# Transposes of branch c's merged sums packed four to a PSUM bank, and the final stores on one queue

## The chip, the core and the metric

One NeuronCore of a Trainium2 chip runs one decoder layer. The metric is device time in microseconds (us), the median of several executions. Engines are called PE (TensorE), ACT (ScalarE), DVE (VectorE), POOL (GpSimd) and SP (SyncE); each runs its own instruction stream in order, and semaphores join them.

## What is computed

The layer works on 256 tokens of width 2048 in float32. A mixer runs three token mixers a, b, c on the normalised input; each result is projected to width 2048, weighted by sigmoid gates and summed; the sum is projected once more and added to the input. A SwiGLU block and a last norm follow.

```python
m = (g[:, :, 0] * (ya @ w_br_a) + g[:, :, 1] * (yb @ w_br_b) + g[:, :, 2] * (yc @ w_br_c))
h = h + m @ w_out
h = h + (silu(rms(h) @ w_gate) * (rms(h) @ w_up)) @ w_down
out = rms_norm(h, norm_final)
```

## The kernel before

Every product is made in split precision: an operand is cut into a rounded high half (ACT, line 108) and the remainder (DVE, line 109) by `split`, and three matmuls stand for one (high by high, low by high, high by low). Weights come from HBM by SP's queue, 1 MB at a time, are cut in SBUF slots, and are multiplied in units. An ordinary unit (`KTiles`, lines 344 to 349) has 24 matmuls of 512 columns; the gates and the SwiGLU use a scheme with fewer products (`Squares`, line 451), whose units have 24 (kind N), 9 (kind Wp) or 12 (kind Ws) matmuls.

`run` writes out the order of the work by hand. Before it emits unit j it emits the cuts of units some way ahead; after the unit it calls `step_side`, which advances one of the waiting generators (`beside`) by one step. So every engine sees its part of a side step between the work of two units, and keeps that order.

Branch c is the third branch (b = 2). Its groups run as: gates of columns 0 and 1 as one `Squares` group, `br(0)`, `br(1)`, gates of columns 2 and 3 as one `Squares` group, `br(2)`, `br(3)`, then the four `output` groups that multiply by `w_out`. When `br(n)` ends, `after` (line 852) adds the gated product to the sums `m[n]` and puts the generator `turn` (line 846) beside the units. `turn` transposes the four 128-column K-tiles of `m[n]`, each for both halves of the tokens (t = 0, 1), so that they can be the stationary operand of `output`. It has two steps of two K-tiles. Each K-tile goes through `transposed` (line 245), which takes a PSUM bank, writes two transposes into half of it (line 249) and splits that half into the slabs of `mT` (lines 108 and 109, 128x256). Over n = 0 to 3 that makes eight steps, called T1 to T8 below: T1 and T2 (n = 0) and T3 and T4 (n = 1) fall between the units of the second gate group, T5 to T8 around `br(3)` and the first `output` group.

PSUM has eight banks, and all tiles of PSUM come from one pool of eight (`bank`, line 93). The pool hands out the bank that was released longest ago in program order; a tile is released when its last reader is done, and the first instruction that writes the new tile waits for that. A `Squares` group holds up to seven banks: a unit N opens four, the first Wp a fifth, the first Ws two more; they stay open until the group nears its end. The unit order of the second gate group is N, Wp, [T2], Ws, [T3], N, Wp, [T4], Ws and so on, with T1 ahead of the first Wp.

```python
def transposed(dst, srcs, scale=None):
    pt = bank()
    for t in range(NT):
        nc.tensor.transpose(pt[:, toks(t)], srcs[t], ident)
    split(*dst, pt[:, :SEQ], scale)
```

At the very end `final_norm` (line 997) is called for the first 128 tokens and then for two column halves of the other 128. When a token tile is done, its four column blocks are scaled, in the order 0, 1, 3, 2: blocks 0 and 3 by DVE (line 1016) and 1 and 2 by ACT (line 1018). Each is stored at once (line 1019, 256 KB): blocks 0 and 3 from SP's queue, 1 and 2 from ACT's.

Of the kernel before, what the change touches and what calls it, by code (L numbers as in the profile page):

```python
# [16 lines left out]
P = 128  # L17
# [13 lines left out]
NT = SEQ // P  # L31
# [20 lines left out]
def trunk(ctx: ExitStack, tc: tile.TileContext, x, norm_mix, norm_ffn, w_in, w_pool, pool_scale,  # L52
          w_br_a, w_br_b, w_br_c, w_out, w_gate, w_up, w_down, rel_bias, norm_final, out):
    nc = tc.nc
    x, out = x[0], out[0]
# [16 lines left out]
    def name(s):  # L72
        uid[0] += 1
        return f"{s}_{uid[0]}"

    def slot(shape, dt=F32):
        return slots.tile([P] + shape, dt, tag="slot", name=name("slot"))
# [4 lines left out]
    def open_late():  # L82

        early_ctx.close()
        late.append(ctx.enter_context(tc.tile_pool(name="late", bufs=3)))

    def wk(dt=F32):
        return work.tile([P, CH], dt, tag="wk", name=name("wk"), bufs=8)
# [4 lines left out]
    def bank():  # L93
        return psum.tile([P, CH], F32, tag="bank", name=name("bank"))

    def f32(ap):
        return ap.bitcast(F32)

    def cols(n):
        return slice(n * CH, (n + 1) * CH)  # L100

    def toks(t):
        return slice(t * P, (t + 1) * P)

    def split(hi, lo, src, scale=None):

        if scale is None:
            nc.scalar.activation(hi, src, AF.Copy)  # L108
            nc.vector.tensor_tensor(lo, src, f32(hi), OP.subtract)  # L109
        else:  # L110
            nc.scalar.activation(hi, src, AF.Copy, scale=scale)
            nc.vector.scalar_tensor_tensor(lo, src, scale, f32(hi), OP.mult, OP.subtract)
# [90 lines left out]
    ident = const.tile([P, P], F32, name="ident")  # L203
# [41 lines left out]
# [6 lines that stand above are left out]
# [14 lines left out]
    def beside(gen, after=2, lag=2):  # L265
        side.append([clock[0] + after, lag, gen])
# [13 lines left out]
    def finish_side():  # L280
        while side:
            clock[0] += 1
            step_side()
# [509 lines left out]
    mT, h, hT = [], [], []  # L793
    gates, m = {}, []
# [35 lines left out]
    def br(n, b, plain=False):  # L830
        key = ("ya", "yb", "yc")[b]

        def lhs():
            y = live[key]
            return lambda kt: (y[0][:, kt, :], y[1][:, kt, :])

        def before():
            if n == 0 and b == 0:
                finish_side()
                open_late()  # L840
                beside((xT.add_differences(p) for p in range(KT // 2)), after=4, lag=2)
            if n % 2 == 0 and b == 0:
                both = slot([2, NT, CH])
                m.extend([both[:, i, t] for t in range(NT)] for i in range(2))

        def turn():
            for j in range(4):
                transposed(mT[0](4 * n + j), [m[n][t][:, j * P:(j + 1) * P] for t in range(NT)])
                if j % 2:
                    yield  # L850

        def after(acc):
            if b == 2 and n == 0:
                mT.append(Halves())
            for t in range(NT):
                g = gates[n][t]
                if plain:
                    nc.scalar.activation(g, g, AF.Sigmoid)
                if b == 0:
                    nc.vector.tensor_mul(m[n][t], acc[t], g)  # L860
                else:
                    nc.vector.tensor_mul(g, acc[t], g)
                    nc.vector.tensor_add(m[n][t], m[n][t], g)
            if b == 2:
                beside(turn(), after=4 if n < 2 else 2, lag=1)

        return Group(lhs, range(HEADS), w_br[b], 0, n * CH, after, before, span=4 if b else 2)
# [98 lines left out]
    def down(part, n):  # L966
        f0, f1 = PARTS[part]
        last = part == len(PARTS) - 1
        cs = cols(n)

        def lhs():
            def tile(kt):
                assert kt // 4 in ready
                return act[kt // 4][:, kt % 4, :], act[kt // 4][:, 4 + kt % 4, :]
            return tile

        def before():
            if last and n == 0:
                load_gf()
                nc.scalar.preload_act_table(AF.Sqrt)  # L980

        def after(acc, t=None, c=slice(0, CH)):
            if t is not None:
                return final_norm(acc, t, c)
            for t in range(NT):
                nc.vector.tensor_add(h[t][:, cs], acc[t], h[t][:, cs])  # L986
                if last:
                    square_sum(st3[:, t, n:n + 1], h[t][:, cs])
                    nc.vector.tensor_mul(h[t][:, cs], h[t][:, cs], gf[0][:, cs])
            if last and n == 2:  # L990
                nc.vector.tensor_reduce(st3[:, :, 4], st3[:, :, 0:3], AX.X, OP.add)
                nc.vector.tensor_scalar(st3[:, :, 4], st3[:, :, 4], 1.0 / D_MODEL, EPS, OP.mult, OP.add)

        return Group(lhs, range(4 * f0, 4 * f1), w_down, f0 * CH, n * CH, after, before, staggered=last and n == 3,
                     span=4)

    def final_norm(acc, t, c):

        hc = h[t][:, 3 * CH + c.start:3 * CH + c.stop]
        a = [st3[:, t, k:k + 1] for k in range(10)]  # L1000
        nc.vector.tensor_add(hc, acc[:, c], hc)
        nc.scalar.activation(wk()[:, c], hc, AF.Square, accum_out=a[3])
        nc.vector.tensor_mul(hc, hc, gf[0][:, 3 * CH + c.start:3 * CH + c.stop])
        if c.stop < CH:
            nc.vector.scalar_tensor_tensor(a[4], a[3], 1.0 / D_MODEL, a[4], OP.mult, OP.add)
            return
        nc.scalar.activation(a[6], a[3], AF.Sqrt, scale=1.0 / D_MODEL, bias=a[4])
        nc.vector.scalar_tensor_tensor(a[5], a[3], 1.0 / D_MODEL, a[4], OP.mult, OP.add)
        nc.vector.reciprocal(a[7], a[6])
        nc.vector.scalar_tensor_tensor(a[8], a[7], a[7], a[5], OP.mult, OP.mult)  # L1010
        nc.vector.tensor_scalar(a[8], a[8], -0.5, 1.5, OP.mult, OP.add)
        nc.vector.tensor_mul(a[9], a[7], a[8])
        for n in (0, 1, 3, 2):
            hn = h[t][:, cols(n)]
            if n in (0, 3):
                nc.vector.tensor_scalar(hn, hn, a[9], None, OP.mult)
            else:
                nc.scalar.activation(hn, hn, AF.Copy, scale=a[9])
            (nc.sync if n in (0, 3) else nc.scalar).dma_start(out[toks(t), cols(n)], hn)

    groups = qkv("a", 0, start_block)
    groups += [channels("u", 3 * WIDTH, c, start_pooling if c else None) for c in range(2)]
# [7 lines left out]
    for part, (f0, f1) in enumerate(PARTS):  # L1030
        for f in range(f0, f1):
            groups += [swiglu(f, f == f1 - 1)]
        k = 2 if f1 - f0 > 2 else 3
# [43 lines left out]
```

## Time and profile before

| | us |
|---|---|
| median of 3 runs | 1565.94 |
| lowest, highest | 1565.84, 1566.08 |
| the profiled execution | 1565.91 |
| its span in the trace | 1564.1 |
| PE busy in the span | 1545.4 |
| DVE busy | 1093.8 |
| ACT busy | 746.3 |

The span runs from the first to the last instruction of the trace; the device time of that execution is 1.8 us longer. A row of the timeline gives start, duration, engine, line, operation, the tiles written and read, the shape and how many instructions were merged; in brackets stands the idle time before the row and what ended it. PEld is the loading of the stationary operand, which runs beside PE's matmuls.

### The profile page before, as it was taken

To read this page: it belongs to the slowest core of one execution; us is meant where nothing else is said; L and a number is where in the kernel's file an instruction comes from. 1 tells how busy PE (TensorE), PEld (TensorE's weight loads), DVE (VectorE), ACT (ScalarE), POOL (GpSimd) and SP (SyncE) were. 2 spreads that over 40 slices of the span, in tenths; PEclk is the share of its full clock that TensorE was granted. 3 is DMA by queue.
4 is the path that set the end of the run, shared out by engine and by line. 5 is a ranking of instruction groups with operands and counts; after the bars stand their busy time and mean duration, and the time that the engine had idled before them with its cause. 6 is when DMAs were issued, how large, how long until landed. Compare 5 with 4: busy or idle time off the path is not lost.

```text
span 1564.1 us, 19170 instructions
## 1 busy us (share of the span) xinstructions
PE 1545.4 (99%) x7895; PEld 1322.9 (85%) x7895; DVE 1093.8 (70%) x1064; ACT 746.3 (48%) x726; POOL 25.9 (2%) x94
## 2 busy tenths in 40 slices
PE   9999999999999999989999999999999999999997
PEld 9998999988888888878888878888888888888886
DVE  6453665644578888867666898667886769857685
ACT  7324343446545544635455545443554345544353
POOL 2000000101100000000000000000000000000000
PEclk9999999999999999999999999999999999999999
DMA  9655455554545655736654566555665555655551
GB/s 352 215 189 165 145 182 176 169 186 137 189 162 191 239 172 205 269 108 244 214 175 163 200 215 215 189 170 181 214 219 190 183 188 189 242 188 164 213 215 54
DMA packets 144456, 300.13 MB, mean 192 GB/s; under 512 B 6464, under 2 KB 8048, under 8 KB 144240
## 3 DMA queue, kind: packets, MB, share of 16 engines
q1 hardware_dynamic: 143024, 296.39, 55.6%
q10 hardware_dynamic: 1040, 1.45, 0.3%
q8 instruction: 62, 1.02, 0.3%
q0 software_dynamic: 304, 1.06, 0.2%
q14 instruction: 26, 0.21, 0.0%
HBM read 296.77 MB, written 2.11 MB: 191 GB/s over the span
## 4 chain that ended last, share of the span: by engine, by line
PE 96%; DVE 2%; ACT 1%; issue 0%; DMA 0%; ACTq 0%; DVEq 0%
PE bank L451 38%; PE bank L344 13%; PE bank L345 13%; PE bank L349 13%; PE bank L364 5%; PE bank L372 5%; PE bank L366 5%; DVE slot L109 1%; PE bank L951 1%; ACT slot L108 1%; PE bank L249 0%; PE bank L596 0%; DMA slot<-in_x_dram 0%; PE bank L597 0%; DVE slot L433 0%
## 5 line engine op out<-in xcount | busy, mean ns | idle before, releaser
L109 DVE TENSOR_TENSOR slot<-slot,slot 128x2048 fp32r<-128x2048 f32 (+3 forms) x406 | 719.0, 1798 | 187.3 <-ACT slot L108 186.8
L108 ACT ACTIVATE slot<-slot 128x2048 fp32r<-128x2048 f32 (+3 forms) x406 | 600.8, 1516 | 339.8 <-DVE slot L435 135.9
L451 PE MATMUL bank<-slot,slot 128*128 128x512 f32 x1719 | 441.3, 391 | 0.0
L451 PEld LDWEIGHTS bank<-slot,slot 128*128 128x128 f32 x1719 | 323.4, 189 | 67.0
L344 PE MATMUL bank<-slot,slot 128*128 128x512 f32 (+1 forms) x936 | 364.4, 390 | 0.0
L345 PE MATMUL bank<-slot,slot 128*128 128x512 f32 (+1 forms) x936 | 362.3, 388 | 0.0
L451 PE MATMUL bank<-slot,late 128*128 128x512 f32 x1014 | 279.4, 390 | 0.0
L349 PE MATMUL bank<-slot,slot 128*128 128x512 f32 (+1 forms) x936 | 236.5, 387 | 0.0
L451 PEld LDWEIGHTS bank<-slot,late 128*128 128x128 f32 x1014 | 189.6, 188 | 39.3 <-DVE slot L109 0.2
L344 PEld LDWEIGHTS bank<-slot,slot 128*128 128x128 f32 x936 | 175.8, 188 | 35.3
L345 PEld LDWEIGHTS bank<-slot,slot 128*128 128x128 f32 x936 | 175.9, 188 | 35.1
L349 PEld LDWEIGHTS bank<-slot,slot 128*128 128x128 f32 x936 | 174.9, 188 | 35.9
L364 PE MATMUL bank<-slot,slot 128*128 128x256 f32 x640 | 158.6, 286 | 0.0
L366 PE MATMUL bank<-slot,slot 128*128 128x256 f32 x640 | 156.9, 283 | 0.0
L366 PEld LDWEIGHTS bank<-slot,slot 128*128 128x128 f32 x640 | 122.8, 192 | 0.0
L364 PEld LDWEIGHTS bank<-slot,slot 128*128 128x128 f32 x640 | 122.7, 192 | 0.1
L372 PE MATMUL bank<-slot,slot 128*128 128x256 f32 x640 | 89.8, 283 | 0.0
L108 ACT ACTIVATE slot<-bank 128x512 fp32r<-128x512 f32 (+1 forms) x46 | 23.3, 520 | 132.0 <-PE bank L951 67.8
L372 PEld LDWEIGHTS bank<-slot,slot 128*128 128x128 f32 x640 | 82.6, 192 | 0.0
L109 DVE TENSOR_TENSOR slot<-bank,slot 128x512 fp32r<-128x512 f32 (+1 forms) x46 | 26.9, 595 | 59.4 <-ACT slot L108 59.4
L433 DVE TENSOR_TENSOR slot<-slot 128x1024 f32<-128x1024 f32 x49 | 59.7, 1218 | 0.0
L986 DVE TENSOR_TENSOR slot<-bank,slot 128x512 f32<-128x512 f32 x30 | 19.6, 686 | 55.5 <-PE bank L349 55.5
(160 smaller groups left out, 630.3 us busy)
## 6 DMA issues: line engine op xcount, KB each, us to landing
slot<-in_w_in_dram SPq DMA_DIRECT2D x103, 1024.0 KB, 5.1
slot<-in_w_gate_dram SPq DMA_DIRECT2D x88, 512.0 KB, 3.9
slot<-in_w_up_dram SPq DMA_DIRECT2D x88, 512.0 KB, 4.8
slot<-in_w_down_dram SPq DMA_DIRECT2D x44, 1024.0 KB, 5.1
slot<-in_w_out_dram SPq DMA_DIRECT2D x16, 1024.0 KB, 5.1
slot<-in_w_br_a_dram SPq DMA_DIRECT2D x8, 1024.0 KB, 5.1
slot<-in_w_br_b_dram SPq DMA_DIRECT2D x8, 1024.0 KB, 5.1
slot<-in_w_br_c_dram SPq DMA_DIRECT2D x8, 1024.0 KB, 5.1
```

Source lines behind the costliest of these rows:

```text
L108: nc.scalar.activation(hi, src, AF.Copy)
L109: nc.vector.tensor_tensor(lo, src, f32(hi), OP.subtract)
L344: nc.tensor.matmul(acc[:, c], hi[:, toks(t)], whi[:, j, c], start=i + j == 0, stop=False)
L345: nc.tensor.matmul(acc[:, c], lo[:, toks(t)], whi[:, j, c], start=False, stop=False)
L349: nc.tensor.matmul(acc[:, c], hi[:, toks(t)], wlo[:, j, c], start=False, stop=i + j == n - 1)
L364: nc.tensor.matmul(o, whi[:, j, w], hi, start=i + j == 0 and c % 2 == 0, stop=False, skip_group_check=True)
L366: nc.tensor.matmul(o, whi[:, j, w], lo, start=False, stop=False, skip_group_check=True)
L372: nc.tensor.matmul(o, wlo[:, j, w], hi, start=False, stop=i + j == n - 1 and c % 2 == 1, skip_group_check=True)
L433: nc.vector.tensor_tensor(s[:, 0:2], raw[:, 0:1].to_broadcast([P, 2, CH]), raw[:, 1:3], OP.add)
L451: nc.tensor.matmul(g.banks[b], x, w[:, k, :], start=start, stop=g.left[b] == 0)
L951: nc.tensor.transpose(pt[:, i * SEQ + t * P:i * SEQ + (t + 1) * P], c[t][1][:, (2 * k + i) * P:(2 * k + i + 1) * P], ident)
L986: nc.vector.tensor_add(h[t][:, cs], acc[t], h[t][:, cs])
```

## The change

`turn` no longer calls `transposed`. A step takes one bank, writes the four transposes of its two K-tiles into its four quarters, and splits the whole bank (128x512) into the pair of slabs at once. The number and the order of the transposes are the same; a step has one bank, one high half and one remainder where it had two of each. The eight final stores are all issued from SP's queue.

```diff
         def turn():
-            for j in range(4):
-                transposed(mT[0](4 * n + j), [m[n][t][:, j * P:(j + 1) * P] for t in range(NT)])
-                if j % 2:
-                    yield
+            for i in range(2):
+                pt = bank()
+                for j in range(4):
+                    c = (2 * i + j // 2) * P
+                    nc.tensor.transpose(pt[:, j * P:(j + 1) * P], m[n][j % 2][:, c:c + P], ident)
+                split(*mT[0].pair(2 * n + i), pt.rearrange("p (k s) -> p k s", k=2))
+                yield
...
-            (nc.sync if n in (0, 3) else nc.scalar).dma_start(out[toks(t), cols(n)], hn)
+            nc.sync.dma_start(out[toks(t), cols(n)], hn)
```

`pair(p)` (line 138) gives the high and the low slab of K-tiles 2p and 2p + 1 as [128, 2, 256] views of the same slot that `mT[0](kt)` indexes singly.

## Rows read from the trace of the kernel before

**Rows 1.** The page: busy time by engine, and GB/s in 40 slices.
```profile
PE 1545.4 (99%) x7895; PEld 1322.9 (85%) x7895; DVE 1093.8 (70%) x1064; ACT 746.3 (48%) x726; POOL 25.9 (2%) x94
...
GB/s 352 215 189 165 145 182 176 169 186 137 189 162 191 239 172 205 269 108 244 214 175 163 200 215 215 189 170 181 214 219 190 183 188 189 242 188 164 213 215 54
```

**Rows 2.** Waits of PE, whole span: who for whom, us, times, longest.
```profile
PE bank L249 <- DVE slot L109: 6.1, 2, 5.2
```

**Rows 3.** Timeline of PE, 685 to 709 us.
```profile
685.74 0.60 PE L249 MATMUL bank<-ident,slot 128*128 128x128 f32 x4
686.09 1.18 PE L451 MATMUL bank<-slot,slot 128*128 128x512 f32 x4
...
688.26 0.60 PE L249 MATMUL bank<-ident,slot 128*128 128x128 f32 x4
...
691.53 0.38 PE L249 MATMUL bank<-ident,slot 128*128 128x128 f32 x2
697.09 0.69 PE L249 MATMUL bank<-ident,slot 128*128 128x128 f32 x2 [5.18 <-DVE slot L109]
697.43 2.91 PE L451 MATMUL bank<-slot,slot 128*128 128x512 f32 x6
...
708.46 0.44 PE L249 MATMUL bank<-ident,slot 128*128 128x128 f32 x2 [0.93 <-DVE slot L109]
708.65 1.63 PE L451 MATMUL bank<-slot,late 128*128 128x512 f32 x6
```

**Rows 4.** Chain that ended last, 600 to 820 us: start, duration, work.
```profile
697.78 9.53 PE bank L451 x33
...
708.90 23.16 PE bank L451 x102
```

**Rows 5.** Windows of 1 us: busy by engine, then PEclk, DMA share, GB/s.
```profile
698.00:699.00 1.00, 1.00 (x4) 0.80 (x3) 0.42 (x1) 1.00 (x2) 0.00 (x0) 0.50 0.31 123
...
702.00:703.00 1.00, 1.00 (x6) 0.82 (x5) 0.32 (x1) 0.00 (x0) 0.00 (x0) 1.00 0.00 0
```

**Rows 6.** Timeline of DVE, 689 to 731 us.
```profile
689.09 0.76 DVE L109 TENSOR_TENSOR slot<-bank,slot 128x256 fp32r<-128x256 f32 x2 [1.77 <-ACT slot L108]
...
696.62 0.41 DVE L109 TENSOR_TENSOR slot<-bank,slot 128x256 fp32r<-128x256 f32 x1
...
709.35 0.42 DVE L109 TENSOR_TENSOR slot<-bank,slot 128x256 fp32r<-128x256 f32 x1 [0.95 <-ACT slot L108]
...
721.27 8.90 DVE L109 TENSOR_TENSOR slot<-slot,slot 128x2048 fp32r<-128x2048 f32 x4 [0.37 <-ACT slot L108]
```

**Rows 7.** Lines 108 and 109 from a bank: ns min/median/max, first and last start.
```profile
L108 ACT ACTIVATE slot<-bank x46: 366/589/601, 181.9 to 1527.2; 128x512 fp32r<-128x512 f32 x30, 128x256 fp32r<-128x256 f32 x16
...
L109 DVE TENSOR_TENSOR slot<-bank,slot x46: 411/684/695, 183.1 to 1527.9; 128x512 fp32r<-128x512 f32 x30, 128x256 fp32r<-128x256 f32 x16
```

**Rows 8.** Timeline of PE and PEld around T8, 771 to 774 us.
```profile
771.42 0.60 PE L249 MATMUL bank<-ident,slot 128*128 128x128 f32 x4
...
773.49 0.19 PEld L344 LDWEIGHTS bank<-slot,slot 128*128 128x128 f32 x1
773.72 0.19 PEld L345 LDWEIGHTS bank<-slot,slot 128*128 128x128 f32 x1
```

**Rows 9.** Timeline of the tail, 1554 to 1560 us.
```profile
1554.10 0.64 PE L349 MATMUL bank<-slot,slot 128*128 128x256 f32 x4
1554.31 0.42 ACT L1002 ACTIVATE wk<-slot 128x256 f32<-128x256 f32 x1 [0.43 <-ACT slot L1018]
...
1555.27 0.42 DVE L1001 TENSOR_TENSOR slot<-bank,slot 128x256 f32<-128x256 f32 x1
...
1559.44 0.34 ACTq L1019 DMA_DIRECT2D out_dram<-slot  x1
```

**Rows 10.** A window of the last stores, and their issues (KB each, us to landing).
```profile
1560.00:1561.00 1.00, 0.00 (x0) 0.00 (x0) 0.00 (x0) 0.00 (x0) 0.00 (x0) 0.50 1.06 309
...
out_dram<-slot SPq DMA_DIRECT2D x4, 256.0 KB, 2.6
```

## The prediction

> **What bounds the kernel now.** I read the page first: PE is busy for 1545.4 of 1564.1 us, DVE for 1093.8 and ACT for 746.3 [rows 1]. Only what frees PE of work, of waits or of a slow clock can shorten the kernel, and what the change saves on DVE and ACT counts only where PE waits for them. So the next view is the list of PE's waits over the whole span. Its longest entry is one that the change touches: PE's transposes of line 249 waited 6.1 us for the remainder of `split` on DVE, twice, once for 5.2 us [rows 2]. The timeline of PE says where. T1 and T2 show four transposes in one row; T3 shows two at 691.53, then 5.18 us of idle time, then the other two at 697.09; the second half of T4 waited 0.93 us [rows 3].
>
> Why these two steps: ahead of T3 the first Ws unit has opened its two banks, so seven of eight are held by the gate products. One bank is left. The first K-tile of T3 takes it, and the second K-tile must wait until ACT and DVE have split the first. That split stands on DVE behind the cut of a whole unit, at 696.62 [rows 6]. T4 meets the same single bank, but finds DVE idle, and loses only the round trip.
>
> The idle time has a second price. After it the matmuls run slowly: 33 of them take 9.53 us [rows 4], where 102 undisturbed ones take 23.16, or 0.227 each. The granted clock says why: 0.50 at 698 to 699 us and 1.00 at 702 to 703 [rows 5]. PE was at the lower of its two levels (1.2 of 2.4 GHz) for some us after the 5.18 us of idleness.
>
> **The change part by part. The steps T3 and T4.** With one bank to a step no second bank is waited for. What remains is counted from undisturbed rows. From T1 to T2 lie four transposes and a Wp unit of 9 matmuls: 688.26 - 685.74 = 2.52 us, and from T1's start to the next matmul 0.35 us [rows 3]. From T3 to T4 lie four transposes and 33 matmuls, so 2.52 + 24 x 0.227 = 7.97 us; then 0.35 to the first matmul after T4. That is 8.32 us. Before, it was 708.65 - 691.53 = 17.12 us [rows 3]. The gain is **8.80 us**: 6.11 of idle time and 2.69 of slow clock. If the clock fell all the same, or something else held the splits, 6.1 would be the lower end.
>
> Does the single bank now hold up the step itself? The new split covers 128x512. Nearest rows: from a bank ACT's median is 0.589 us and DVE's 0.684, most of them of this size [rows 7]; their destinations are contiguous, here they are two strips of 256, which I price the same. The gaps between PE, ACT and DVE were together 0.07 us at T4 (709.35 - 708.46 - 0.44 - 0.38) [rows 3, 6, 7]. So a step ends on DVE 0.60 + 0.07 + 0.59 + 0.68, some 2.0 us after its first transpose. T2's bank is free at 690.3, and T3 asks for it at 691.5: 1.2 us to spare. T3's split, behind the same unit's cut on DVE at 696.6 and 0.5 later through T2, ends by 697.8; T4 would ask at 691.53 + 7.97 = 699.5: 1.7 us to spare.
>
> **What waits behind the new split.** ACT now waits for four transposes where it waited for two, and behind it on ACT and DVE stand the cuts of the next units. After T4 DVE is done 2.0 - 0.35 = 1.65 us after the next matmul has begun; before it was 709.77 - 708.65 = 1.12. The cuts come 0.5 us later against PE. The tightest of them is the Ws unit that is cut first in the row at 721.27: done at 721.27 + 8.90 / 4 = 723.5 [rows 6]; the unit begins 66 matmuls after 708.90, at 723.9, and needs this half after 8 more, at 725.7 [rows 4]. Of 2.2 us 1.7 remain. So PE should run on.
>
> **T5 to T8** have banks enough and no waits in the list, and their transposes stay as they are. The danger is the end of the new split. T8 starts at 771.42, so the high half is there at 772.7 and the remainder at 773.4; PE loads K-tile 14's at 773.49 and 773.72 [rows 8]. It fits by 0.8 and 0.3 us; the step before it also serves the unit that follows at once, with the same margins. I cost it at nothing; if ACT or DVE is 0.3 us late there, up to 0.3 us each time.
>
> **Saved instructions.** Eight steps have one split of 512 in place of two of 256. That frees some 0.1 us per step on ACT and DVE, nothing that PE waits for: no gain.
>
> **The stores.** Two issues leave ACT's stream while the first token tile is finished, each with 0.43 us of idle time on ACT [rows 9]. So the square of line 1002 can start up to 0.86 us before 1554.31, and DVE's line 1001 at 1555.27, which stood behind what that square feeds, moves up with it until PE's last matmuls hold it: 1554.10 + 0.64 = 1554.74 [rows 9]. That is **0.50 us**, and all that follows is one chain. After that the last four stores are 1.05 MB at 309 GB/s with the DMA engines full [rows 10]: 3.4 us from the first store on, whatever queue issues them. At the 352 GB/s of the page's first slice [rows 1] it would be 3.0, so the tail gains 0.9 at best; at worst, if the single queue eats the half us, nothing. SP's issue of the four, one by one, still ends before 1559.44, where ACT issued the last [rows 9].
>
> The sum: 8.80 + 0.50 = 9.30. The profiled execution took 1565.91 us, of which 1.8 lie around the span, and 1565.91 is the median to 0.03 us: **1556.6 us**. With both ends of the terms, 1555.7 to 1559.3.
>
> **The rivals.** First, *DVE becomes the bound*. PE comes 8.8 us earlier to cuts which DVE and ACT made in part while PE stood still. If they cannot be made earlier, because a slot or a load comes at its old time, PE waits again after T4, in short pieces; only the 6.1 us of idle time or less and the tail are gained: 1559.3. Against it: the slots are freed by PE's own units, and 1.7 us are to spare.
>
> Second, *the lost overlap*. While a bank is being written, its first half can't be read; each step's split starts one pair of transposes (0.60 - 0.38 = 0.22 us [rows 3]) later, and if each of eight steps passed it on to PE, 1.8 us would go back: 1558.4. For it: T8 and the step before it, with 0.3 us to spare. Against it: T2 and T3 with 1.2 and 1.7. The Trainium skill says this as a rule in Perfetto Trace Analysis, section Matmuls: independent groups should rotate through different banks, so that one is emptied while the next is filled. By that rule two banks a step are better, and the sum would be 1558.4; in T3 the trace disagrees, since with one bank free there was nothing to rotate to, and the rotation cost 5.18 us.
>
> Third, *the change does not do what it says*: the bank that T3 gets is still being split, so the wait moves from the second half to the first, and only the tail gains: 1565.4. Against it: the split of T2 ended on DVE at 689.09 + 0.76 = 689.85 [rows 6], 1.7 us ahead of T3.
>
> Fourth, the one that ends slower: *the single queue works its stores off one after another*. A store alone takes 2.6 us to land [rows 10]. The first tile's four would need 10.4 us and have 5.1 until the second tile's (1554.31 to 1559.44 [rows 9]), 5.3 too many; the last four would take 10.4 in place of 3.4. That is 12.3 lost against 9.3 gained: 1568.9. It decides from 2.2 us a store on (8 stores less 5.1 and 3.4). Against it: 256 KB in 2.6 us are 101 GB/s, and the weights, which come by this very queue, reach 352 [rows 1].
>
> **How the numbers follow.** Forecast 0.78, DVE the bound 0.08, lost overlap 0.05, no effect 0.05, single queue 0.04. The range from 1555.6 (the better tail) to 1558.8 holds the forecast and the lost overlap, and half of the first rival. A measurement of this kernel tells 0.2% (3.1 us) from no change: faster is the forecast, the first and the second rival, 0.91; same 0.05; slower 0.04.
>
> **What would show it.** In the profile after, PE's list of waits has no line 249 on DVE in the second gate group; T3 and T4 are rows of four transposes 8.0 us apart; the granted clock stays at 1.00 from 690 to 710 us; all later units come 8.8 us earlier; line 1001 starts just after PE's last matmul. I am wrong if a wait on DVE line 109 comes up at another matmul between T4 and the end of the gate group, if the units of `output` behind the last two steps are held up, or if the last store lands more than 3.5 us after the first.

## The result, and the profile after

The kernel after takes 1556.63 us (median of 6 runs, 1556.37 to 1557.08), the kernel before 1565.89 beside it (1565.35 to 1566.19). The ratio is 0.9942, with a 95% interval of 0.9929 to 0.9954: 9.3 us less. The forecast was 1556.6. Beside each other once more, on the second chip of the experiments, the two stood at 1556.74 and 1565.69, ratio 0.9943 (0.9931 to 0.9956). The span of the profiled execution is 1555.3 us where it was 1564.1.

PE's waits in the kernel after, whole span (who for whom, us in total, times, longest), answer to [rows 2]:

```profile
PE bank L217 <- POOL ident masks.py:199: 1.4, 1, 1.4
PE bank L954 <- DVE wk L947: 1.2, 2, 0.8
PE bank L249 <- DMA slot<-in_x_dram: 0.2, 1, 0.2
```

The transposes of the merged sums, now line 851, are not among them; line 249 is left with the transposes of x at the start. The timeline of PE, to be laid beside [rows 3] (its last row is T8, for [rows 8]):

```profile
691.99 0.60 PE L851 MATMUL bank<-ident,slot 128*128 128x128 f32 x4
...
699.97 0.60 PE L851 MATMUL bank<-ident,slot 128*128 128x128 f32 x4
700.32 1.63 PE L451 MATMUL bank<-slot,late 128*128 128x512 f32 x6
...
745.32 0.60 PE L851 MATMUL bank<-ident,slot 128*128 128x128 f32 x4
...
763.08 0.60 PE L851 MATMUL bank<-ident,slot 128*128 128x128 f32 x4
```

The row at 745.32 is T5. In the kernel before it was

```profile
753.66 0.60 PE L249 MATMUL bank<-ident,slot 128*128 128x128 f32 x4
```

T3 and T4 are whole rows of four, 7.98 us apart, and no idle time stands at either. In this execution PE reached T1 0.53 us later than in the one shown of before (686.27 against 685.74), so distances count, not positions: from T3 to the first matmul after T4 it is 8.33 us, where it was 17.12.

The chain that ended last (start, duration, work) answers to [rows 4], and the window (busy by engine, then PEclk, DMA share, GB/s) to [rows 5]:

```profile
692.60 7.53 PE bank L451 x33
...
700.57 23.15 PE bank L451 x102
```

```profile
698.00:699.00 1.00, 1.00 (x6) 0.84 (x5) 1.00 (x2) 0.00 (x0) 0.00 (x0) 1.00 1.00 414
```

The 33 matmuls that took 9.53 us take 7.53, and the granted clock is 1.00 in the window that had 0.50. The other rows of DVE, for [rows 6], and the row of PEld that takes T8's remainder, for [rows 8]:

```profile
697.53 0.68 DVE L109 TENSOR_TENSOR slot<-bank,slot 128x512 fp32r<-128x512 f32 x1
698.13 2.28 DVE L109 TENSOR_TENSOR slot<-slot,slot 128x2048 fp32r<-128x2048 f32 x1
...
701.24 0.69 DVE L109 TENSOR_TENSOR slot<-bank,slot 128x512 fp32r<-128x512 f32 x1 [0.82 <-ACT slot L108]
...
711.29 1.75 DVE L109 TENSOR_TENSOR slot<-slot,slot 128x1536 fp32r<-128x1536 f32 x1
713.42 8.90 DVE L109 TENSOR_TENSOR slot<-slot,slot 128x2048 fp32r<-128x2048 f32 x4 [0.38 <-ACT slot L108]
...
764.35 0.69 DVE L109 TENSOR_TENSOR slot<-bank,slot 128x512 fp32r<-128x512 f32 x1 [1.82 <-ACT slot L108]
```

```profile
765.37 0.19 PEld L345 LDWEIGHTS bank<-slot,slot 128*128 128x128 f32 x1
```

And the tail, for [rows 9], with a window and the issues of the stores, for [rows 10]:

```profile
1545.74 0.64 PE L349 MATMUL bank<-slot,slot 128*128 128x256 f32 x4
1546.42 0.42 DVE L1004 TENSOR_TENSOR slot<-bank,slot 128x256 f32<-128x256 f32 x1 [0.47 <-PE bank L349]
```

```profile
1551.00:1552.00 1.00, 0.00 (x0) 0.00 (x0) 0.00 (x0) 0.00 (x0) 0.00 (x0) 0.50 1.11 318
...
out_dram<-slot SPq DMA_DIRECT2D x8, 256.0 KB, 3.1
```

DVE's addition now follows PE's last matmul by 0.04 us (1546.38 to 1546.42) and names PE as what it waited for. Before it began 0.53 us behind it [rows 9]. From PE's last matmul to the end of the span it is 8.90 us; it was 9.37 (1554.74 to 1564.11).

### The profile page after: what moved, and what is told of

Its sections match the earlier page's. It is cut to its first block, busy times and chain, and to the rows that moved or that the text cites. A ratio compares the mean times of both kernels' runs of the same rounds, so it can differ in the third digit from the quotient of the medians.

```text
span 1555.3 us, 19158 instructions
## 1 busy us (share of the span) xinstructions
PE 1543.5 (99%) x7895; PEld 1322.2 (85%) x7895; DVE 1093.0 (70%) x1056; ACT 745.4 (48%) x718; POOL 25.8 (2%) x94
## 4 chain that ended last, share of the span: by engine, by line
PE 97%; DVE 1%; ACT 0%; issue 0%; DMA 0%; ACTq 0%; DVEq 0%
PE bank L451 38%; PE bank L344 14%; PE bank L345 14%; PE bank L349 14%; PE bank L364 5%; PE bank L372 5%; PE bank L366 5%; DVE slot L109 1%; PE bank L954 1%; PE bank L596 0%; DMA slot<-in_x_dram 0%; ACT slot L108 0%; PE bank L597 0%; PE bank L851 0%; PE bank L907 0%
## 5 line engine op out<-in xcount | busy, mean ns | idle before, releaser
L108 ACT ACTIVATE slot<-bank 128x512 fp32r<-128x512 f32 x38 | 22.6, 594 | 123.5 <-PE bank L954 67.8
L109 DVE TENSOR_TENSOR slot<-bank,slot 128x512 fp32r<-128x512 f32 x38 | 26.2, 689 | 54.0 <-ACT slot L108 54.0
```

## The experiments

The theory: the second bank of T3 and T4 was the wait, 6.1 us of it; the idle time cost 2.7 us more by PE's clock; the stores give 0.5 us because ACT is free between the token tiles. Each experiment takes one of these apart or bounds one of the margins. To be free of where PE's work happens to start, distances of the trace are compared beside the times: T3 to T5 (62.13 us before, 53.33 after) and the tail (9.37 and 8.90). The runs e1 to e6, e8 and e9 were made on one chip, e7 and e10 to e12 on a second. The kernel before took 1565.70 us on the first and 1565.69 on the second. The kernel after was timed on the second only, so on the first e1, which differs from it in the stores alone, stands in for it.

### The two halves of the change, each alone

```diff
# e1_transposes_alone, against the kernel after
-            nc.sync.dma_start(out[toks(t), cols(n)], hn)
+            (nc.sync if n in (0, 3) else nc.scalar).dma_start(out[toks(t), cols(n)], hn)
# e2_stores_alone, against the kernel before
-            (nc.sync if n in (0, 3) else nc.scalar).dma_start(out[toks(t), cols(n)], hn)
+            nc.sync.dma_start(out[toks(t), cols(n)], hn)
```

> The steps of the transposes as in the change, the stores as before. My theory (the second bank of T3 and T4 was waited for, and the idle time let PE's clock fall): 8.8 us of the gain are here, 1565.9 - 8.8 = 1557.1 us; T3 and T4 are rows of four transposes 8.0 us apart, the tail is as long as before (9.4 us from PE's last matmul to the end of the span). Rival (part of the gain comes from the stores in a way that the sum missed): under 8 us of gain, 1558 or more.

> The stores as in the change, the transposes as before. My theory: the tail is 0.5 us shorter because ACT, without two issues between its instructions, lets DVE's line 1001 follow PE's last matmul at once: 1565.4 us, and the trace shows line 1001 0.03 us behind PE. Rival (the single queue is what helps or hurts): a difference other than 0.5 us, and a distance from the last scaling to the end of the span that is not the 6.56 us of before.

The transposes alone: 1557.03 us (1556.89 to 1557.51), ratio 0.9944 (0.9930 to 0.9958), 8.7 us of gain. T3 and T4 in PE's timeline, and DVE's line 1004 in the tail:

```profile
691.62 0.60 PE L851 MATMUL bank<-ident,slot 128*128 128x128 f32 x4
...
699.59 0.60 PE L851 MATMUL bank<-ident,slot 128*128 128x128 f32 x4
...
1545.40 0.64 PE L349 MATMUL bank<-slot,slot 128*128 128x256 f32 x4
...
1546.58 0.42 DVE L1004 TENSOR_TENSOR slot<-bank,slot 128x256 f32<-128x256 f32 x1
```

T3 to T4 is 7.97 us, T3 to T5 53.32; the addition comes 0.54 us after PE again, and the tail is 9.40 us. The stores alone: 1565.25 us (1564.96 to 1565.75), against 1565.70, ratio 0.9997 (0.9988 to 1.0006). The time by itself does not tell that from no change; the trace does. PE's wait and the tail:

```profile
PE bank L249 <- DVE slot L109: 6.1, 2, 5.2
```

```profile
1553.68 0.64 PE L349 MATMUL bank<-slot,slot 128*128 128x256 f32 x4
1554.36 0.42 DVE L1001 TENSOR_TENSOR slot<-bank,slot 128x256 f32<-128x256 f32 x1 [0.47 <-PE bank L349]
```

The old wait is there, 6.1 us as in [rows 2], the addition follows PE at once, and the tail is 8.85 us. From ACT's last scalings to the end of the span it is 6.52 us (6.56 in the kernel before), so the half us lies ahead of the stores. The two halves add up to the whole and do not touch each other.

### Which of the stores matter

```diff
# e5_first_tile_on_sp, against the kernel after
+            (nc.sync if t == 0 or n in (0, 3) else nc.scalar).dma_start(out[toks(t), cols(n)], hn)
# e6_last_tile_on_sp
+            (nc.sync if t == 1 or n in (0, 3) else nc.scalar).dma_start(out[toks(t), cols(n)], hn)
```

> As the kernel after, but only the first token tile's four stores are all on SP's queue; of the second tile's, blocks 1 and 2 are issued from ACT again. My theory (the gain of the tail is that ACT is free between the tiles): from PE's last matmul to the end of the span as long as in the kernel after, 8.9 us. Rival (the last four stores gain from one queue): 9.4 us.

> The converse: the first tile's blocks 1 and 2 from ACT as before, the second tile's four stores all on SP. My theory: 9.4 us from PE's last matmul to the end of the span, as before. Rival (one queue helps the last stores): 8.9 us.

One run each: 1556.92 and 1557.73 us. The second half's addition in the tail of the first, then two rows of the tail of the second:

```profile
1546.37 0.42 DVE L1004 TENSOR_TENSOR slot<-bank,slot 128x256 f32<-128x256 f32 x1 [0.47 <-PE bank L349]
```

```profile
1546.16 0.42 ACT L1005 ACTIVATE wk<-slot 128x256 f32<-128x256 f32 x1 [0.43 <-ACT slot L1021]
...
1547.12 0.42 DVE L1004 TENSOR_TENSOR slot<-bank,slot 128x256 f32<-128x256 f32 x1
```

With the first tile's stores off ACT the tail is 8.89 us; with only the last tile's, ACT's square waits 0.43 us behind an issue again and the tail is 9.35. All of the half us comes from ACT between the tiles. That the last four stores share a queue changes nothing: in the trace's packets they take 3.35 to 3.39 us from first to last in before, after, e5 and e6 alike.

### The clock's share

```diff
# e4_busy_while_waiting, against the kernel before (cut: a constant tile `zero`, and `pairs`, which keeps the gate groups)
             for j in range(4):
+                if n == 1 and j == 1:
+                    rhs = xT.parts[0][:, 0].rearrange("p a s -> p (a s)")
+                    for _ in range(20):
+                        nc.tensor.matmul(pairs[1, 2].banks[2], zero, rhs, start=False, stop=False)
                 transposed(mT[0](4 * n + j), [m[n][t][:, j * P:(j + 1) * P] for t in range(NT)])
```

> The kernel before with 20 added matmuls of a zero operand (128x512, adding zero to a bank of the gate products that is open) between the two halves of T3, where PE stood idle for 5.18 us. They fill 20 x 0.227 = 4.5 us of it. The waits on the bank stay, only the idleness goes. My theory (2.7 us of the 8.8 are the clock that fell after the idle time): the 33 matmuls after T3 take 7.5 us rather than 9.53, and the kernel 1565.9 - 2.5 = 1563.4 us. Rival (the matmuls after T3 are slow for another reason, such as loads of their weights): still 9.5 us for the 33 and 1565.9 us.

1563.54 us (1563.40 to 1564.21), against 1565.70: ratio 0.9987 (0.9978 to 0.9996). Twenty matmuls more, and 2.2 us less. PE's waits, its timeline (T3, and T5 in the last row), a window of the clock and the chain:

```profile
PE bank L249 <- DVE slot L109: 1.6, 2, 0.9
```

```profile
691.47 0.38 PE L249 MATMUL bank<-ident,slot 128*128 128x128 f32 x2
691.61 4.79 PE L836 MATMUL bank<-slot,zero 128*128 128x512 f32 x20
697.04 0.44 PE L249 MATMUL bank<-ident,slot 128*128 128x128 f32 x2 [0.64 <-DVE slot L109]
...
751.35 0.60 PE L249 MATMUL bank<-ident,slot 128*128 128x128 f32 x4
```

```profile
698.00:699.00 1.00, 1.00 (x6) 0.81 (x5) 0.35 (x1) 1.00 (x1) 0.00 (x0) 1.00 0.94 336
```

```profile
697.48 7.54 PE bank L451 x33
```

The second half of T3 still starts 5.57 us after the first (5.56 in the kernel before), since the bank comes free no sooner. But PE was not idle for 5 us, the granted clock stayed at 1.00, and the 33 matmuls took 7.54 us. So the slow matmuls were the idle time's second price, and weights that came late are ruled out.

The run also measures that price. T3 to T5 is 59.88 us here: 2.25 less than the 62.13 of the kernel before, which is the clock, and 6.55 more than the 53.33 of the kernel after, which is what the two waits cost. That is 0.44 more than the 6.11 of idle time in PE's list. So the 8.80 us divide into 6.55 and 2.25, and not into 6.11 and 2.69.

The size of the clock's part is not the same in each execution. In the run of the stores alone, where the same wait stands, the 33 matmuls took 8.70 us and not 9.53, and T3 to T5 61.29 and not 62.13:

```profile
698.20 8.70 PE bank L451 x33
```

```profile
698.00:699.00 1.00, 1.00 (x4) 0.81 (x4) 0.34 (x1) 0.76 (x2) 0.00 (x0) 0.50 0.60 242
...
701.00:702.00 1.00, 1.00 (x6) 0.78 (x5) 1.00 (x1) 0.00 (x0) 0.00 (x0) 1.00 0.00 0
```

There the clock was back at 1.00 a us earlier than in the kernel before, whose window from 701 to 702 us still shows 0.53. By the same reckoning the clock cost 1.41 us in this execution (2.25 - 0.84). The runs of the kernel before also spread wider (1564.51 to 1566.84 us in 9 on the second chip) than those of the kernel after beside them (1556.50 to 1556.95 in 5). Each run's mean granted clock goes with it: of 21 runs of the kernel before on the first chip, the 14 with a mean of 0.996 have a median of 1566.24 us and the 7 with 0.997 one of 1565.10, and the ten of e4, at 0.998 and 0.999, lie between 1563.40 and 1564.21. So the clock goes with much of that spread. What decides how long it stays low stays open; two traces of it were read.

### One bank, but two splits

```diff
# e3_one_bank_two_splits, against the kernel after
-                split(*mT[0].pair(2 * n + i), pt.rearrange("p (k s) -> p k s", k=2))
+                for k in range(2):
+                    split(*mT[0](4 * n + 2 * i + k), pt[:, k * SEQ:(k + 1) * SEQ])
```

> As the kernel after, but each step's bank is split in two halves of 128x256, as before, so the instructions that the change saves on ACT and DVE are back. My theory (the bank alone matters): the same time as after, 1556.6 us, within 0.3. Rival (fewer instructions on DVE and ACT carry part of the gain): later, up to the 0.1 us per step and engine, so 1557.4 at most; if DVE is the bound by then, waits of PE on line 109 come up between T4 and the end of the gate group.

1557.26 us (1557.19 to 1557.66), outside what I expected. On the same chip e1 took 1557.03, with a tail that is 0.52 us longer than the one here (9.40 against 8.88), so the two splits cost some 0.7 us. T3 to T4 is 7.97 us, so the bank does all that was claimed for it there. But T3 to T5 is 54.19, 0.86 longer. PE has a new wait, and ACT and DVE show where it is from (timelines behind T3 and T4, which began at 691.39 and 699.36):

```profile
PE bank L451 <- DVE slot L109: 0.4, 1, 0.4
```

```profile
697.77 0.38 ACT L108 ACTIVATE slot<-bank 128x256 fp32r<-128x256 f32 x1 [2.43 <-DVE slot L109]
...
702.65 0.39 ACT L108 ACTIVATE slot<-bank 128x256 fp32r<-128x256 f32 x1 [2.27 <-DVE slot L109]
```

```profile
699.99 2.29 DVE L109 TENSOR_TENSOR slot<-slot,slot 128x2048 fp32r<-128x2048 f32 x1 [1.38 <-ACT slot L108]
...
703.07 0.42 DVE L109 TENSOR_TENSOR slot<-bank,slot 128x256 fp32r<-128x256 f32 x1 [0.45 <-ACT slot L108]
703.41 1.22 DVE L433 TENSOR_TENSOR slot<-slot 128x1024 f32<-128x1024 f32 x1
```

ACT's copy of the second half waits until DVE is done with the first half of the same bank. With two banks it followed the first copy at once, as at T2 in the kernel before:

```profile
688.68 0.66 ACT L108 ACTIVATE slot<-bank 128x256 fp32r<-128x256 f32 x2 [1.86 <-PE bank L249]
```

So the halves go ACT, DVE, ACT, DVE in turn. (The wait is one of the program's semaphores; no run shows what the chip would do without it.) At T3 DVE reaches the first half only behind the cut of a whole unit, ACT's second copy waits 2.43 us for it, and what stands behind that copy on ACT, the high half of the next unit, comes late. DVE's part of that unit starts 8.60 us after T3 (699.99 - 691.39), where it was 6.14 in the kernel after (698.13 - 691.99), and T4's split stands behind it. DVE reaches the next sums 4.05 us after T4's start; in the kernel after it is 1.87 (701.84 - 699.97). Of these 2.18 us PE feels 0.86. So the single split of 512 is a needed part of the change, for the order that it spares: the instructions that it saves, some 0.1 us a step, don't make 2.18.

### How much DVE has to spare

```diff
# e8_dve_late (16 additions) and e12_dve_late_4 (4), against the kernel after
                 split(*mT[0].pair(2 * n + i), pt.rearrange("p (k s) -> p k s", k=2))
+                if n == 1 and i == 1:
+                    for _ in range(16):
+                        nc.vector.tensor_tensor(ones, ident, ident, OP.add)
                 yield
```

> As the kernel after, with 16 small additions of 128x128 on DVE behind T4's split, some 2.5 to 3 us of DVE's time that nobody reads. They stand ahead of the cuts of the next units. My theory (1.7 us to spare at the tightest cut): PE waits on line 109 or 108 some 1 to 1.5 us in all between T4 and the end of the gate group, 1557.6 to 1558.1 us, and the rest is hidden. Rival (DVE is the bound there already): the whole 2.5 to 3 us show, 1559.1 or more. Second rival (DVE has much more to spare): no wait, 1556.6.

> The kernel after with 4 small additions on DVE behind T4's split. In the run with 16 they took 5.18 us, so here about 1.3; 3.8 of the 5.1 us by which the cuts then came later showed in PE's time, so 1.3 to 1.7 are to spare. My theory: no wait of PE, or under 0.2 us, and the time of the kernel after. Rival (every us on DVE shows, DVE is the bound): 1.3 us slower.

With 16: 1560.43 us (1560.17 to 1562.60), much above the 1557.6 to 1558.1 that I gave. The trace is of the longest of the six runs, which reached T1 some 2 us later than the others' traces, so it is read by distances. PE's waits, its timeline, and DVE's:

```profile
PE bank L451 <- DVE slot L109: 2.9, 2, 1.7
```

```profile
713.14 0.73 PE L451 MATMUL bank<-slot,slot 128*128 128x512 f32 x2 [1.22 <-DVE slot L109]
...
720.01 0.72 PE L451 MATMUL bank<-slot,slot 128*128 128x512 f32 x2 [1.69 <-DVE slot L109]
```

```profile
703.65 5.18 DVE L855 TENSOR_TENSOR ones<-ident 128x128 f32<-128x128 f32 x16
708.75 1.22 DVE L433 TENSOR_TENSOR slot<-slot 128x1024 f32<-128x1024 f32 x1
```

The additions took 5.18 us and not 2.5 to 3; that was the miss. The sums began 5.10 us later against T4 than in the kernel after, and T3 to T5 grew by 3.78 us (57.11): 1.3 us were absorbed. With 4 additions the sums began 1.19 us later, no wait of PE on DVE's cuts came up, T3 to T5 is 53.33 and the time 1556.86 us (1556.74 to 1557.21). In the run with two splits 1.3 were absorbed as well (2.18 - 0.86).

The later stop here, and the only one in the run with two splits, stand 63 matmuls after T4, at the remainder of the second Wp unit. In the kernel after that remainder is done at 711.29 + 1.75 = 713.04, and PE comes to it at

```profile
714.71 0.62 PE L451 MATMUL bank<-slot,slot 128*128 128x512 f32 x2
```

So 1.67 us are to spare there. Cuts that are 1.2 us late cost nothing; those that were 2.18 and 5.10 late each cost 0.35 us more than what goes beyond 1.67.

### The margin of the one bank, and the lost overlap

```diff
# e9_t4_one_unit_earlier, against the kernel after
-                yield
+                if n or not i:
+                    yield
# e7_two_banks_from_t5, against the kernel after
             for i in range(2):
+                if n > 1:
+                    for j in range(2 * i, 2 * i + 2):
+                        transposed(mT[0](4 * n + j), [m[n][t][:, j * P:(j + 1) * P] for t in range(NT)])
+                    yield
+                    continue
```

> As the kernel after, but T2's generator ends with its second step, so that T4 comes one unit earlier, after the unit N that follows T3, only 5.8 us behind T3 and not 8.0. My theory (T4 needs the one bank, which T3's split gives back about 6.2 us after T3 began, behind a unit's cut on DVE): PE waits for line 109 at the first transpose of T4, for 0.3 to 0.8 us; the time is 1556.9 to 1557.4 us, and the clock does not fall. Rival (the bank is free all the time): no wait and 1556.6 us.

> As the kernel after, but T5 to T8 take two banks and two splits each, as before. My theory (the lost overlap costs nothing there, since the new split ends 0.3 us before PE needs it): the same as the kernel after on this chip, within 0.2 us, and T5 to T8 at the same distances in both (5.94, 5.91, 5.92 us). Rival (one bank a step holds PE up where banks are free): up to 0.3 us at two steps faster than after.

T4 one unit earlier: 1557.02 us (1556.86 to 1557.71), and in PE's timeline

```profile
691.68 0.60 PE L851 MATMUL bank<-ident,slot 128*128 128x128 f32 x4
...
697.96 0.66 PE L851 MATMUL bank<-ident,slot 128*128 128x128 f32 x4 [0.19 <-DVE slot L109]
```

The wait is there, less than I gave (0.19 us; 6.28 from T3 to T4 where 5.93 is undisturbed, as from T5 to T6; T3 to T5 is 53.72, 0.39 longer). So the bank returns about 6.2 us after T3 has begun, and the kernel after, which comes back for it at 7.98, has 1.7 us in hand.

Two banks from T5 on: 1556.97 us (1556.38 to 1557.21) beside 1556.74 (1556.50 to 1556.95); T5 to T8 at 5.93, 5.91 and 5.92 us in both. Where banks are free one bank a step costs nothing, and two gain nothing. The rule on rotating banks that the prediction weighed (the Trainium skill, Perfetto Trace Analysis, section Matmuls) would have made this run faster; here it neither gains nor costs, as the split ends 0.3 us before PE needs it.

> The kernel after once more, beside the others of this call on one chip: 1556.6 to 1557.0 us, as the two runs that differ from it in the stores alone or hardly at all. It is there so that differences of half a us are taken on one chip.

The kernel after once more gave 1556.74 us, as used above.

### A try for a shorter tail

```diff
# e11_first_block_early, against the kernel after; line 1006 moves behind this
+        for k in range(2):
+            hk = h[t][:, k * SEQ:(k + 1) * SEQ]
+            nc.vector.tensor_scalar(hk, hk, a[9], None, OP.mult)
+            nc.sync.dma_start(out[toks(t), k * SEQ:(k + 1) * SEQ], hk)
...
-        for n in (0, 1, 3, 2):
+        for n in (1, 3, 2):
```

> The kernel after, with a shorter way to the first store: the first column block of a token tile is scaled in two halves of 256 columns, each stored by itself, and the product of line 1006 stands behind it on DVE instead of ahead of the statistics. My theory (the end is the first store plus 3.4 us of transfers with the DMA engines full): the first packet leaves 0.2 to 0.4 us earlier and the tail from PE's last matmul is 8.5 to 8.7 us, not 8.9. Rival (what ends the tail is the last store's issue or the number of stores, five in place of four): 8.9 us or more.

1556.48 us (1556.40 to 1556.97) beside 1556.74: no difference that can be told. The tail is 8.87 us, not 8.5 to 8.7. In the trace's packets the first of the last tile left 3.46 us after PE's last matmul and not 3.67, as expected, but from there to the last packet it took 3.61 us and not 3.38. The issues:

```profile
out_dram<-slot SPq DMA_DIRECT2D x6, 256.0 KB, 2.9
out_dram<-slot SPq DMA_DIRECT2D x4, 128.0 KB, 1.9
```

What the early start gave, the transfers took back. Between 1549.30 and 1550.55 us the DMA engines were not full (at most 0.91 busy in any quarter of a us), where in the kernel after they are full from the second quarter on. Two things differ: the half blocks move in packets of 1 KB where whole ones move in 2 KB, and SP issues five stores one after another instead of four. This run doesn't tell them apart, so the rival that I named is not ruled out. I had the first store set the end, with a fixed time behind it; that time is not fixed when the stores are cut differently.

## Why the prediction was right

**What bounds the kernel.** The list of PE's waits had one long entry, and it is the one that went. Nearly all of the gain lies in two places, T3 to T5 (62.13 to 53.33 us, 8.80 less) and the tail (9.37 to 8.90, 0.47 less); the span is only 8.83 shorter, mainly because PE happened to reach T1 0.53 us later in the profiled run.

**T3 and T4.** 8.32 us were forecast from T3 to the first matmul after T4, 8.33 were measured. The gain of 8.80 came out too, since it was the difference of two distances. Its division into 6.11 of idle time and 2.69 of slow clock was wrong: e4 gives 6.55 for the two waits and 2.25 for the clock, so each stop of PE cost some 0.2 us more than the idle time in its list, and the prediction had put all that was left down to the clock. The clock's part is not a constant either: it was 1.41 in the other trace. That the forecast met the time to 0.03 us is in part luck: it was worked out from one execution, which lay at the median, and the same two kernels were 9.26 us apart in one comparison and 8.95 in the other.

**The margins.** DVE is done with T4's split 1.61 us after the next matmul began (1.65 forecast). The cut that I called the tightest ends at 713.42 + 8.90 / 4 = 715.65 and is needed 74 matmuls after 700.57, at 717.4: 1.7 us, as forecast. Ahead of it the second Wp unit has no more, 1.67, and where cuts came late, it was there that PE stopped. At least 1.2 us of it can be used without loss. At T8 the remainder is there at 765.04, 0.33 us before PE loads it at 765.37 (0.3 forecast).

**The tail.** 0.50 was forecast, 0.47 measured, by the way that was named: ACT's two issues between the tiles. Neither bound was needed; the queue of the last stores moved nothing. The bounds of the sum were added up wrongly, though: with 0.9 for the tail in place of 0.50 the lower one is 1556.2 us, not 1555.7, and with nothing for it the upper one is 1559.8, not 1559.3. The time lies within either pair.

**The rivals.** DVE was no bound: 1.2 us more of its work cost nothing, and 2.18 us of delay would have cost 0.86. The lost overlap is nil (e7). The wait did not move to the first half (T3 has none; it would come at a distance of 6.2 us, e9). The single queue works its stores off together, 3.35 us for four.

What else I had wrong did not enter the sum: the saved instructions. I set them at a tenth of a us per step and hidden. As one bank with two splits they would have cost some 0.7 us (0.86 in the trace), because ACT and DVE take turns on a bank in this program.

## What to carry to other kernels

When a long accumulation holds all but one bank, count the banks that a side task takes per step: the second one waits for a whole round of the engines that empty the first, behind whatever stands in their queues, and PE's idle time is paid twice when the clock falls with it. Pack what fits into one bank and empty it by one instruction per engine: with two, ACT and DVE took turns on the bank here, and the second turn waited 2.43 us behind other work. A DMA issued from ACT's stream held ACT's next instruction back by 0.43 us here, so look at what stands behind it, not at how many queues share the transfers.

## What the runs showed of the hardware that was not expected

After the same idle time of 5.18 us, PE's clock came back at different times in two executions: 33 matmuls took 9.53 us in one and 8.70 in the other, against 7.53 without the idle time. In the first the granted clock fell at 695.1 us, while PE stood idle, and was back at 701.9; in the other it fell at 697.2 and was back at 700.6. Added matmuls of no use made a kernel 2.2 us faster (e4).
